# The delta rule's output projection starts in the branch's own pool, and the output weights load in another order

## The chip, the cores and the metric

The kernel runs on one NeuronCore of one Trainium2 chip. The core has a matrix engine (TensorE; its weight loads are listed apart as PEld), a vector engine (VectorE, in the profile DVE), a scalar engine (ScalarE, ACT), GpSimd (POOL) and a sync engine (SP), which issues the DMA transfers here. TensorE writes its sums into PSUM banks of 128 x 512 float32. The metric is the time of one execution on the device in microseconds; 2331.53 us is the median of three runs before the change (2330.88 to 2333.11).

## The reference

Two layers of a decoder trunk over 512 tokens of width 1024, in float32. Each layer normalises x and feeds three branches side by side: a Mamba-2 state space branch, a latent attention (MLA) and a gated delta rule (GDN). Each branch's result is projected to the model width and gated, the three are added and projected once more, and a feed-forward part follows:

```
mixed = g_ssd * (y_ssd @ w_ssd_out) + g_mla * (y_mla @ w_mla_out) + g_gdn * (y_gdn @ w_gdn_out)
h = x + mixed @ w_out
f = jnp.square(jax.nn.relu(rmsnorm(h, norm2_g) @ w_up)) @ w_down
return h + f
```

The gates are sigmoids of a projection of the normalised x. The change touches `g_gdn * (y_gdn @ w_gdn_out)`, `mixed @ w_out` and, through a shared helper, the product with `w_down`.

## The kernel before, in words

**Products.** A float32 operand is split into a high part, rounded to fp32r, and a low rest; three matmuls (L182 high by high, L183 low by high, L184 high by low, or the other way round) make one product. `weights` loads a weight block of 512 KB into one of two buffers `wraw` (L161) and splits it 512 columns at a time, on ScalarE (L154, `whi`) and VectorE (L155, `wlo`), into a ring of four pairs. One such pair feeds 12 matmuls of 512 columns where two feature tiles are computed. `dense_F` runs one product with the features on the partitions: it takes one bank for each of its two feature tiles from the four accumulation banks `acc`.

**The branches.** In order of the text come the state space groups, the attention's projection in between, the delta rule's matrices, the state space branch's projection (`out_proj`), and two calls of `gdn_unit`, each for four heads. A unit walks four chunks of 128 tokens: a chain that alternates between TensorE (L1004 to L1042), VectorE (L1008 to L1045), ScalarE (L1051) and GpSimd (the power of L259) and ends with four multiplies on VectorE into the tile `gz` (L1063; its buffers have the tag `tok`). After the four chunks, four features are transposed one after another through a single bank (`y_bank`, L1068) and split into `yh` and `yl` (L254, L255), the operands of the delta rule's projection.

**`out_proj`** goes over pairs of feature tiles, `dp` 0 to 3. For each pair it computes the gate logits (`dense_F` of `xh`, `xl` with a slice of w_in), takes a tanh of each bank into a gate tile (L464), computes the branch's projection (`dense_F` of `yh`, `yl` with w_gdn_out), multiplies it on to the gate tile (L473) and adds that to `mixed` (L474). The gate tile is a buffer `cva` of the given pool, or what `make` gives; with `make`, L473 and L474 have a raised priority.

**Pools over one another.** The branches' tiles lie in the pool `br`, closed after the second unit. The pools `hp` (the residual `h`, 2 MB) and `wo` (the output product) are opened afterwards over the same memory; a tile in them waits until the tiles of `br` that it overlaps have been read for the last time. Before the change all of the delta rule's projection comes behind that point: pairs 0 to 2 at once, with gate tiles in places of `wo` and `hp` that are not in use yet (`slots`), and pair 3 inside the output product (`mid`).

**The output product.** `seven` multiplies with w_out (and later four times per layer with w_down) as 2 x 2 blocks with seven block products (Strassen's scheme in Winograd's form): a11, a12, s2, s1, s3, s4, a22. `seven_weights` gives the four blocks of 1 MB, `wr00`, `wr01`, `wr11` and `wr10`, loaded by `after(c)` for c = 0, 1, 2, 3 in that order (L1113), and two sums of blocks on VectorE (L1107): `wp1` = block 00 + block 01, and block 01 += block 11. Each sum is two additions of 128 x 1024. A third sum (L1159) builds the operand of the product s2 from `wp1` and block 11, a fourth (L1170) that of a22. For w_down, `after(c)` is called behind the c-th of four column groups of the up projection.

**Order.** A planner orders each engine's instructions ahead of time: it goes through a simulated time and takes the instruction that comes first in the text among those that are ready and have a buffer, or one of raised priority. It can so take an instruction well ahead of its place in the text. On the chip each engine, and the DMA queue of SP, then works through its list in that fixed order.

Of the kernel before, what the change touches and what calls it, by code (L numbers as in the profile page):

```python
# [55 lines left out]
def hybrid_kernel(ctx, tc, a, out, depth=2, taps=None):  # L56
# [108 lines left out]
    def weights(w2d, c0, n, K, hold=None, raw0=None):  # L165

        kt = min(1024 // n, K // P)  # L170
        step = 512 // n
        for k0 in range(0, K // P, kt):
            given = raw0 is not None and k0 == 0
            raw = raw0 if given else weights_raw(w2d, c0, n, k0, kt)
            for q in range(0, kt, step):
                hi, lo = split_half(raw[:, q * n : (q + step) * n], hold and hold[k0 + q], not given)
                v = lambda x: x.rearrange("p (k n) -> p k n", n=n)
                yield k0 + q, v(hi), v(lo)
# [7 lines left out]
    def dense_F(gen, cols, K, xh, xl, mid=None, banks=None, after=None):  # L186

        pss = banks or [acc_bank() for _ in cols]
        last = K // P - 1
        if mid:
            gen = list(gen)
            for i, hf in enumerate(HALVES):
                for ps, c in zip(pss, cols):
                    for k0, wh, wl in gen:
                        for k in range(wh.shape[1]):  # L200
                            kk = k0 + k
                            mm3(ps[:, hf], wh[:, k, c], wl[:, k, c], xh[kk][:, hf], xl[kk][:, hf], kk == 0, kk == last)
                if i == 0:
                    mid()
            return pss
        for k0, wh, wl in gen:
            for ps, c in zip(pss, cols):
                for k in range(wh.shape[1]):
                    a_, b_ = wh[:, k, c], wl[:, k, c]
                    mm3(ps[: a_.shape[1], :], a_, b_, xh[k0 + k], xl[k0 + k], k0 + k == 0, k0 + k == last)  # L210
            if after:
                after()
        return pss
# [110 lines left out]
    hpl = h_pool.enter_context(tc.tile_pool(name="hp", bufs=1, reuse_waits="tile"))  # L324
# [26 lines left out]
    for ly in range(depth):  # L351
# [107 lines left out]
        def out_proj(w2d, br, yh, yl, pl, part=range(4), after=None, make=None, gate_banks=lambda: None):  # L459
            for dp in part:  # L460
                tg = []
                for j, ps in enumerate(dense_F(weights(w_in, O_GATE + br * D + dp * 256, 256, D), tiles(256), D, xh, xl, None, gate_banks(), after)):
                    t_ = make(dp, j) if make else mk(pl, [P, S], F32, "cva", 2)
                    act.activation(t_, ps, AF.Tanh, scale=0.5)  # L464
                    tg.append(t_)
                for j, ps in enumerate(dense_F(weights(w2d, dp * 256, 256, D), tiles(256), D, yh, yl, after=after)):
                    d = 2 * dp + j
                    if mixed[d] is None:
                        mixed[d] = mk(lp, [P, S], F32, "mix", 8)
                        dve.scalar_tensor_tensor(mixed[d], tg[j], 1.0, ps, ALU.add, ALU.mult)  # L470
                    else:
                        with tc.high_priority() if make else nullcontext():
                            dve.scalar_tensor_tensor(tg[j], tg[j], 1.0, ps, ALU.add, ALU.mult)  # L473
                            dve.tensor_tensor(mixed[d], mixed[d], tg[j], ALU.add)  # L474
# [224 lines left out]
        br = bp.enter_context(tc.tile_pool(name="br", bufs=1, reuse_waits="tile"))  # L699
# [391 lines left out]
        yg = hilo_tags(lp, "y")  # L1091
        for u in range(2):
            gdn_unit(u, *mats[u], *yg)
        bp.close()


        h_pool = ExitStack()
        hpl = h_pool.enter_context(tc.tile_pool(name="hp", bufs=1, reuse_waits="tile"))
        last = ly == depth - 1
        ssq = [mk(sp, [P, 2], F32, "nss", 4) for _ in range(T)]  # L1100
        def seven_weights(pl, w2d, r0):

            b = {}

            def plus(o, x, y):
                for q in (slice(0, 1024), slice(1024, 2048)):
                    dve.tensor_tensor(o[:, q], x[:, q], y[:, q], ALU.add)  # L1107

            def after(c):
                i, j = ((0, 0), (0, 1), (1, 1), (1, 0))[c]  # L1110
                b[i, j] = mk(pl, [P, 4 * 512], F32, f"wr{i}{j}")
                rows, cols = (slice(o + 512 * e, o + 512 * (e + 1)) for o, e in ((r0, i), (0, j)))
                sync.dma_start(b[i, j].rearrange("p (k n) -> p k n", k=4), w2d[rows, cols].rearrange("(k p) n -> p k n", p=P))  # L1113
                if c == 1:
                    b["p1"] = mk(pl, [P, 4 * 512], F32, "wp1")
                    plus(b["p1"], b[0, 0], b[0, 1])
                if c == 2:
                    plus(b[0, 1], b[0, 1], b[1, 1])

            return b, after  # L1120
# [59 lines left out]
            product(x, "a22", of(p4), False, 1, 0, ALU.add, 2)  # L1180

        with tc.tile_pool(name="wo", bufs=1, reuse_waits="tile") as wo:
            slots = {(0, 0): (wo, "wr00"), (0, 1): (hpl, "h"), (1, 0): (wo, "wr10"), (1, 1): (wo, "wp1"),
                     (2, 0): (wo, "wr01"), (2, 1): (wo, "wr11"), (3, 0): (wo, "fs"), (3, 1): (wo, "fs")}

            def gate_tile(dp, j):
                pl, tag = slots[dp, j]
                return mk(pl, [P, S], F32, tag, 2 if tag == "fs" else 1)

            out_proj(a["w_gdn_out"][ly], 2, *yg, wo, (0, 1, 2), make=gate_tile)  # L1190
            h = mk(hpl, [P, T, D], F32, "h")
            for t in range(T):
                sync.dma_start(h[:, t, :], xsrc[t * P : (t + 1) * P, :])
            hts = [h[:, t] for t in range(T)]
            b, after = seven_weights(wo, a["w_out"][ly], 0)
            for c in (0, 3, 1, 2):
                after(c)
            ops = {}
            ck_pair = lambda: list(zip(*hilo_tags(lp, "ck", 2)))
            ops["a11"], ops["s3"] = ck_pair(), list(zip(*hilo_tags(wo, "s3", 2)))  # L1200

            def mid():
                out_proj(a["w_gdn_out"][ly], 2, *yg, wo, (3,), make=gate_tile, gate_banks=lambda: [sm_bank() for _ in range(2)])
                fh, fl = hilo_tags(lp, "x")
                for i, n in enumerate(("a12", "s2", "s1", "s4")):
                    ops[n] = [(fh[2 * i + e], fl[2 * i + e]) for e in range(2)]
                ops["a22"] = ck_pair()

            def put(n, d, s):
                hi, lo = (x[:, d % 2 * 256 : d % 2 * 256 + 256] for x in ops[n][d // 2])  # L1210
                act.mul(hi, s, 0.5)
                dve.scalar_tensor_tensor(lo, s, 0.5, f32(hi), ALU.mult, ALU.subtract)

            def comb(x, y, op):
                s = mk(wo, [P, 256], F32, "fc", 8)
                dve.tensor_tensor(s, x, y, op)
                return s

            half = lambda i: lambda d: mixed[d][:, HALVES[i]]
            t0, t1 = half(0), half(1)  # L1220

            held = []

            def forms(n):
                for d in range(4):
                    with tc.high_priority() if d > 1 and n in ("a12", "s2") else nullcontext():
                        form(n, d)

            def form(n, d):
                if n == "a11":  # L1230
                    put("a11", d, t0(d))
                    put("s3", d, comb(t0(d), t1(d), ALU.subtract))
                if n == "a12":
                    put("a12", d, t0(d + 4))
                if n == "s2":
                    s = comb(t1(d), t1(d + 4), ALU.subtract)
                    s2 = comb(s, t0(d), ALU.subtract)
                    put("s2", d, s2)
                    held.append((s, s2))
                if n == "s1":  # L1240
                    s, s2 = held[d]
                    put("s1", d, s)
                    put("s4", d, comb(t0(d + 4), s2, ALU.add))
                if n == "a22":
                    put("a22", d, t1(d + 4))

            nf = []

            def n2(i, pl, *tag):
                if not nf:  # L1250
                    nf.extend(hilo_tags(lp, "x"))
                norm_half(i, hts, ssq, lambda k: col(g_n2 + k), pl, *nf, *tag)

            seven(wo, ops, b, ssq, lambda: n2(0, wo, "f", 2), nf=2, pre=forms, mid=mid)
            xh, xl = nf
# [138 lines left out]
```

## Time and profile before

| | |
|---|---|
| median of three runs | 2331.53 us |
| the profiled execution | 2332.37 us |
| its span, first to last instruction | 2330.6 us |
| mean granted TensorE clock | 0.993 |
| TensorE busy | 2280.6 us |
| VectorE busy | 1647.8 us |
| ScalarE busy | 1201.1 us |

The profile has one execution. A row of the timeline gives start, duration, engine, line, operation, written and read tiles, their shapes and the number of instructions merged, and in brackets the idle time of the engine just before and what ended it. A row of the waits gives the engine and line that waited, what released it, the total in us, the number of times and the longest. A row of the windows gives the window, its length, then busy time and number of instructions of PE, PEld, DVE, ACT and POOL, the granted clock of TensorE as a share of full speed, the busy share of the DMA engines and their GB/s.

### The profile page before, as it was taken

The numbers are of one execution on the slowest core, as the hardware profiler recorded it, in microseconds if no ns is written. First come the engines' busy times: TensorE is split into PE (matmuls) and PEld (weight loads), VectorE is DVE, ScalarE is ACT, GpSimd is POOL, SyncE is SP. The second block draws the span as 40 slices with busy tenths as digits, with TensorE's granted clock in tenths as the row PEclk, the third lists the DMA queues.
The fourth block names the chain that finished last, engine by engine and source line by source line (L and its number), as shares of the span: only waits on it lengthen the run. The fifth ranks groups of instructions, "written<-read, shape, count | busy, mean of one in ns | idle before, by whom it ended". The sixth has DMA issues, their size and how long they took to land.

```text
span 2330.6 us, 32281 instructions
## 1 busy us (share of the span) xinstructions
PE 2280.6 (98%) x11810; PEld 1873.1 (80%) x11810; DVE 1647.8 (71%) x3256; ACT 1201.1 (52%) x2509; POOL 59.5 (3%) x74
## 2 busy tenths in 40 slices
PE   9999999999998999999999999999999999999998
PEld 7888787878887888888888877878788778888886
DVE  7777566866665868767867775668657649778668
ACT  6666744333443455554657666443344335545545
POOL 0000000000000000000000000000000100000000
PEclk9999999999999999999999999999999989999999
DMA  4223633442224233233132236334422242432231
GB/s 141 79 73 100 191 100 116 145 119 82 79 67 136 90 136 109 82 109 118 52 97 78 78 108 190 100 109 145 119 82 82 63 136 73 145 117 100 91 109 46
DMA packets 220032, 244.16 MB, mean 105 GB/s; under 512 B 34256, under 2 KB 172384, under 8 KB 219872
## 3 DMA queue, kind: packets, MB, share of 16 engines
q1 hardware_dynamic: 219872, 242.09, 34.0%
q8 instruction: 93, 1.52, 0.3%
q14 instruction: 67, 0.55, 0.1%
HBM read 225.60 MB, written 11.74 MB: 102 GB/s over the span
## 4 chain that ended last, share of the span: by engine, by line
PE 87%; DVE 7%; ACT 2%; issue 1%; POOL 1%; DMA 1%; SPq 0%; DVEq 0%; POOLq 0%; ACTq 0%
PE acc L182 22%; PE acc L183 22%; PE acc L184 22%; PE sm L184 2%; PE sm L182 2%; PE sm L183 2%; DVE wlo L155 2%; PE sm L752 1%; DVE tok L880 1%; ACT whi L154 1%; PE sm L650 1%; DVE gQ L879 1%; PE sm L1037 1%; POOL gms L259 1%; PE sm L761 1%
## 5 line engine op out<-in xcount | busy, mean ns | idle before, releaser
L155 DVE TENSOR_TENSOR wlo<-wraw,whi 128x512 fp32r<-128x512 f32 (+1 forms) x536 | 366.1, 686 | 363.5 <-ACT whi L154 358.0
L154 ACT CAST whi<-wraw 128x512 fp32r<-128x512 f32 (+1 forms) x536 | 330.2, 618 | 555.5 <-PE acc L183 380.5
L182 PE MATMUL acc<-xh,whi 128*128 128x512 f32 (+1 forms) x1344 | 522.7, 390 | 0.7 <-ACT xh L254 0.7
L184 PE MATMUL acc<-xh,wlo 128*128 128x512 f32 (+1 forms) x1344 | 523.1, 390 | 0.0
L183 PE MATMUL acc<-xl,whi 128*128 128x512 f32 (+1 forms) x1344 | 522.8, 389 | 0.3 <-DVE xl L255 0.3
L183 PEld LDWEIGHTS acc<-xl,whi 128*128 128x128 f32 x1344 | 253.4, 189 | 48.4 <-DVE xl L255 1.1
L182 PEld LDWEIGHTS acc<-xh,whi 128*128 128x128 f32 x1344 | 252.5, 188 | 49.4 <-ACT xh L254 1.5
L184 PEld LDWEIGHTS acc<-xh,wlo 128*128 128x128 f32 x1344 | 253.4, 189 | 47.5
L154 ACT CAST whi<-wr 128x512 fp32r<-128x512 f32 x168 | 104.4, 621 | 111.0 <-PE acc L183 50.1
L182 PE MATMUL acc<-yh,whi 128*128 128x512 f32 x384 | 152.6, 401 | 1.6 <-ACT yh L254 1.6
L183 PE MATMUL acc<-yl,whi 128*128 128x512 f32 x384 | 153.3, 399 | 0.0
L184 PE MATMUL acc<-yh,wlo 128*128 128x512 f32 x384 | 151.5, 394 | 0.0
L155 DVE TENSOR_TENSOR wlo<-wr,whi 128x512 fp32r<-128x512 f32 x168 | 113.5, 687 | 33.9 <-ACT whi L154 33.1
L691 DVE SCALAR_TENSOR_TENSOR ckl<-acc,pc,ckl 128x511 f32<-128x511 f32 (+2 forms) x168 | 120.3, 743 | 15.5 <-ACT ckl L687 8.2
L182 PEld LDWEIGHTS acc<-yh,whi 128*128 128x128 f32 x384 | 72.9, 191 | 17.3 <-ACT yh L254 2.6
L184 PEld LDWEIGHTS acc<-yh,wlo 128*128 128x128 f32 x384 | 73.1, 190 | 14.6
L183 PEld LDWEIGHTS acc<-yl,whi 128*128 128x128 f32 x384 | 73.4, 191 | 14.0
L183 PE MATMUL acc<-wlo,xh 128*128 128x512 f32 (+1 forms) x208 | 80.1, 385 | 0.0
L184 PE MATMUL acc<-whi,xl 128*128 128x512 f32 (+1 forms) x208 | 79.7, 385 | 0.0
L182 PE MATMUL acc<-whi,xh 128*128 128x512 f32 (+1 forms) x208 | 79.2, 382 | 0.0
L1144 DVE TENSOR_TENSOR h<-h,acc 128x512 f32<-128x512 f32 x120 | 77.2, 681 | 0.2 <-PE acc L184 0.2
L454 ACT ACTIVATE eE<-eE,cum 128x128 f32<-128x128 f32 x192 | 63.2, 390 | 24.6 <-DMA eE<-d_c 19.7
(455 smaller groups left out, 4560.9 us busy)
## 6 DMA issues: line engine op xcount, KB each, us to landing
wraw<-in_w_in_dram SPq DMA_DIRECT2D x144, 512.0 KB, 3.6
wraw<-in_w_up_dram SPq DMA_DIRECT2D x64, 512.0 KB, 3.6
wr<-in_w_down_dram SPq DMA_DIRECT2D x32, 1024.0 KB, 5.3
eE<-d_c SPq DMA_DIRECT2D x48, 256.0 KB, 3.7
wraw<-in_w_mla_out_dram SPq DMA_DIRECT2D x16, 512.0 KB, 3.4
eE<-d_e SPq DMA_DIRECT2D x32, 256.0 KB, 2.8
wraw<-in_w_ssd_out_dram SPq DMA_DIRECT2D x16, 512.0 KB, 3.3
wraw<-in_w_gdn_out_dram SPq DMA_DIRECT2D x16, 512.0 KB, 3.4
```

The lines of the kernel that those rows point to most:

```text
L154: act.copy(hi, raw)
L155: dve.tensor_tensor(lo, raw, f32(hi), ALU.subtract)
L182: pe.matmul(o, ah, bh, start=start, stop=False, skip_group_check=more)
L183: pe.matmul(o, ah, bl, start=False, stop=False, skip_group_check=more)
L184: pe.matmul(o, al, bh, start=False, stop=stop, skip_group_check=more)
L259: pool.tensor_tensor(o, o, (exp if exp is not None else nhalf)[:, : o.shape[1]], ALU.pow)
L454: act.activation(o[:, i], o[:, i], AF.Relu, scale=-1.0, bias=cum[:, t, h0 + i : h0 + i + 1])
L650: pe.transpose(ps[:, n : n + P], pn[t][:, kb * P : (kb + 1) * P], ident)
L691: dve.scalar_tensor_tensor(acc[:, d:], ps[:, : S - d], taps_[3 - d], acc[:, d:], ALU.mult, ALU.add)
L752: pe.matmul(py[64 * i : 64 * i + 64, c * P : (c + 1) * P], xd[:, t, h * 64 : (h + 1) * 64], e2[h // 4][:, h % 4, :], start=True, stop=True)
L761: pe.matmul(po[:, c * P : (c + 1) * P], st[:, c * P : (c + 1) * P], ctl[:, tok], start=True, stop=True)
L1144: dve.tensor_tensor(hs_, hs_, ps[t], op)
```

## The change

The first pair of the delta rule's projection (dp = 0) is computed ahead of the closing of the branch's pool, with its gate tiles in the branch's `cva` buffers and without raised priority. Pairs 1 and 2 stay behind it and get other places for their gate tiles. The blocks of w_out are loaded in the order 00, 01, 11, 10 (before: 00, 10, 01, 11). In `seven_weights`, for w_out and w_down, both sums are written one load later.

```diff
         for u in range(2):
             gdn_unit(u, *mats[u], *yg)
+        out_proj(a["w_gdn_out"][ly], 2, *yg, br, (0,))
         bp.close()
...
-                if c == 1:
+                if c == 2:
                     b["p1"] = mk(pl, [P, 4 * 512], F32, "wp1")
                     plus(b["p1"], b[0, 0], b[0, 1])
-                if c == 2:
+                if c == 3:
                     plus(b[0, 1], b[0, 1], b[1, 1])
...
-            slots = {(0, 0): (wo, "wr00"), (0, 1): (hpl, "h"), (1, 0): (wo, "wr10"), (1, 1): (wo, "wp1"),
-                     (2, 0): (wo, "wr01"), (2, 1): (wo, "wr11"), (3, 0): (wo, "fs"), (3, 1): (wo, "fs")}
+            slots = {(1, 0): (wo, "wr11"), (1, 1): (hpl, "h"), (2, 0): (wo, "wr10"), (2, 1): (wo, "fs"),
+                     (3, 0): (wo, "fs"), (3, 1): (wo, "fs")}
...
-            out_proj(a["w_gdn_out"][ly], 2, *yg, wo, (0, 1, 2), make=gate_tile)
+            out_proj(a["w_gdn_out"][ly], 2, *yg, wo, (1, 2), make=gate_tile)
...
-            for c in (0, 3, 1, 2):
+            for c in range(4):
                 after(c)
```

## The prediction

> **What bounds the kernel now.** I read the busy shares first, then who waited for whom on TensorE, then the order of time around the one large wait, and last the windows.
>
> ```profile
> PE 2280.6 (98%) x11810; PEld 1873.1 (80%) x11810; DVE 1647.8 (71%) x3256; ACT 1201.1 (52%) x2509; POOL 59.5 (3%) x74
> PE yt L1068 <- DVE tok L1063: 9.2, 4, 4.1
> PE sm L1037 <- issue: 3.0, 2, 1.5
> ```
>
> TensorE is busy 98% of the span, so 50 us of idle is all there is, and its largest wait sits where the delta rule's last transposes (L1068) wait for VectorE. It comes once per layer at 4.1 us (the 9.2 us hold two more, small ones). Two windows per layer, in each pair layer 0 first: the tail of the delta rule, and all that follows up to the second norm.
>
> ```profile
> 708.44:726.20 17.76, 11.40 (x47) 8.67 (x46) 7.86 (x20) 5.86 (x16) 1.01 (x1) 0.81 0.09 31
> 1861.05:1880.03 18.98, 12.62 (x47) 9.32 (x46) 7.86 (x20) 5.85 (x16) 1.01 (x1) 0.64 0.08 28
> 726.20:828.68 102.48, 102.48 (x451) 84.22 (x450) 74.27 (x135) 47.05 (x96) 0.96 (x2) 1.00 0.36 118
> 1880.03:1982.50 102.47, 102.46 (x451) 84.24 (x450) 74.19 (x135) 47.16 (x96) 0.97 (x2) 1.00 0.36 118
> ```
>
> In the tail TensorE idles 17.76 - 11.40 = 6.36 us and again 18.98 - 12.62 = 6.36 us, at a mean granted clock of 0.81 and 0.64. Afterwards it has no gap for 102 us, one matmul per 102.48/451 = 227 ns. So the change can win only in the tail, and behind it can only lose. The tail of layer 0 in order of time, TensorE first, then ScalarE, VectorE and the DMA queue:
>
> ```profile
> 696.36 0.48 PE L184 MATMUL acc<-xh,wlo 128*128 128x512 f32 x1
> 696.67 0.40 PE L182 MATMUL acc<-yh,whi 128*128 128x512 f32 x1
> 707.62 0.49 PE L1018 MATMUL sm<-tok,tok 128*128 128x128 f32 x2 [0.41 <-DVE tok L1015]
> 709.94 1.13 PE L1037 MATMUL sm<-wk,eE 128*128 128x128 f32 x8 [1.50 <-issue]
> 716.03 0.33 PE L1068 MATMUL yt<-ct,tok 128*128 128x128 f32 x1 [4.09 <-DVE tok L1063]
> 717.13 1.22 PE L182 MATMUL acc<-yh,whi 128*128 128x512 f32 x2 [0.78 <-ACT yh L254]
> 726.20 0.42 PE L182 MATMUL acc<-xh,whi 128*128 128x512 f32 x1
> ...
> 699.21 0.62 ACT L1025 ACTIVATE wk<-sm,gcd 128x128 f32<-128x128 f32 x2 [3.09 <-DVE wk L1020]
> ...
> 723.71 0.62 ACT L154 CAST whi<-wraw 128x512 fp32r<-128x512 f32 x1 [0.36 <-PE acc L183]
> 725.47 0.59 ACT L464 ACTIVATE wr<-acc 128x512 f32<-128x512 f32 x1
> 725.95 0.60 ACT L464 ACTIVATE h<-acc 128x512 f32<-128x512 f32 x1
> ...
> 708.55 0.69 DVE L155 TENSOR_TENSOR wlo<-wraw,whi 128x512 fp32r<-128x512 f32 x1
> ...
> 686.40 11.63 SPq L161 DMA_DIRECT2D wraw<-in_w_in_dram  x2
> 709.27 0.37 SPq L161 DMA_DIRECT2D wraw<-in_w_gdn_out_dram  x1
> ```
>
> Pair 0's gate products (from xh) end at 696.36 and its projection products (from yh) start at 696.67; the half of them that needs only the first unit's rows fills the delta rule's steps until 708. Then TensorE has nothing it may do. Pair 1's gate weights are there: both loads were issued by 698, and the load at 709.27, into the slot of the first of them, shows its two splits done (the second ends at 708.55 + 0.69). What is missing is banks. Pair 0's gate sums sit in two of the four accumulation banks from 696.8 until their tanh at 725.47 and 725.95, because those tanh write into tiles (wr00, h) that lie over the branch's tiles, which the last transposes still read; the projection holds the other two. Pair 1's first gate matmul starts at 726.20, right behind the first tanh.
>
> **The change part by part.**
>
> *Pair 0's gate tiles in the branch's pool.* Nothing is added: the same 48 + 48 matmuls, 2 tanh, 2 fused multiplies and 2 adds, in two buffers (cva) that the branch has already. Moved is the tanh, some 28 us earlier (to 697, where ScalarE idles 3.09 us ahead of 699.21), and two banks come free there. Pair 1's gate products can then fill the tail: 48 x 0.227 = 10.9 us of work. The tail's loss is its idle time and its slow clock:
>
> ```profile
> 709.50:712.90 3.40, 2.00 (x12) 1.57 (x12) 1.19 (x5) 1.05 (x4) 0.00 (x0) 1.00 0.46 159
> 712.90:716.40 3.50, 0.33 (x1) 0.14 (x1) 1.71 (x9) 0.81 (x7) 1.01 (x1) 1.00 0.01 2
> 716.40:723.10 6.70, 5.97 (x18) 4.85 (x19) 1.86 (x4) 1.81 (x3) 0.00 (x0) 0.50 0.00 0
> 1859.94:1863.35 3.41, 1.62 (x11) 1.34 (x12) 2.51 (x7) 0.55 (x1) 0.00 (x0) 0.99 0.11 30
> 1863.35:1877.00 13.65, 8.79 (x26) 6.47 (x26) 4.42 (x14) 3.74 (x12) 1.01 (x1) 0.50 0.09 31
> ```
>
> Idle: 6.36 + 6.36 = 12.7 us. Half clock: half of the busy time in it, 5.97/2 + 8.79/2 = 7.4 us. Together 20.1 us, 10 per layer, and 10.9 us of filler stand against it. The second half of the filler must be split inside the tail: its raw block has landed, a ring place comes free when the first 12 matmuls are done, and ScalarE is busy 5.86 of 17.76 us, VectorE 7.86.
>
> The order of the queues is fixed by a planner, so the fill won't be exact. Where filler was at hand it fell short by 0.41 us (the row at 707.62). I take that at four places per layer, ahead of L1037, of the first transposes, of the first product behind them and once among the later transposes: 8 x 0.45 = 3.6 us stays. Expected gain 20.1 - 3.6 = 16.5 us. Bounds: 20.1 us if all goes; nothing if the planner doesn't fill.
>
> On the clock, row and page differ. In layer 0 it fell behind a window with 0.33 of 3.50 us busy and held through one with 2.00 of 3.40; in layer 1 it fell behind one with 1.62 of 3.41 busy. So half empty is enough here, and the fill must be dense. The Trainium skill ("TensorE: Matmul & The Clock Gate", Part 1: The HAM clock gate) states that the clock halves after an idle window of about 3.4 us; layer 1 had no such idle time before 1863.35, so the trace agrees only in part. With a dense fill both give the same sum.
>
> *No raised priority* for pair 0's two multiplies and adds (4 x 0.69 us on VectorE): they gate pair 1's projection banks, but pair 1's leftover gate matmuls, 10.9 - 10 = 0.9 us, and the other two banks stand ahead. Between 0 and 0.9 us late per layer; I take 0, as the idle share of VectorE in the tail is over half.
>
> *The tiles move on.* Pair 1 now gets wr11 and h, pair 2 wr10 and fs. Their tanh still wait for the branch's tiles, and then the projection of pair 0 is through anyway. The residual's load into h now waits for pair 1, not pair 0, and block 11 of w_out too; blocks 00 and 01 wait for no gate, block 10 for pair 2.
>
> ```profile
> 734.66 1.45 SPq L1193 DMA_DIRECT2D h<-in_x_dram  x3
> 770.98 2.17 SPq L1113 DMA_DIRECT2D wr<-in_w_out_dram  x2
> 775.04 3.49 SPq L161 DMA_DIRECT2D wraw<-in_w_gdn_out_dram  x2
> 730.00:740.00 10.00, 10.00 (x46) 8.29 (x45) 5.36 (x11) 4.56 (x9) 0.00 (x0) 1.00 0.95 315
> 750.31 0.68 DVE L474 TENSOR_TENSOR mix<-mix,wp 128x512 f32<-128x512 f32 x1
> 776.25 1.28 DVE L1144 TENSOR_TENSOR h<-h,acc 128x512 f32<-128x512 f32 x2
> ```
>
> The residual goes out 16 us later, at 751 on the old clock (pair 1's last add is at 750.31), 2 MB and a block of 1 MB at 315 GB/s land by 761, and the first use is at 776.25: hidden. Queued behind them on the DMA queue are the weights of pair 2's projection. Four splits of 12 matmuls stand ahead of TensorE, 4 x 2.72 = 10.9 us; the burst needs 3 MB/315 = 10 us and the weights 3.4 more. Between 0 and 2.5 us per layer; I take 0, since two such blocks ahead of weights (770.98, then 775.04) cost TensorE nothing.
>
> *The sums one load later.* 40 additions of 1.22 us, 4 per product, none more or fewer:
>
> ```profile
> 778.05 2.35 DVE L1107 TENSOR_TENSOR wp<-wr,wr 128x1024 f32<-128x1024 f32 x2
> 770.00:780.00 10.00, 10.00 (x46) 8.29 (x45) 9.97 (x18) 4.47 (x9) 0.00 (x0) 1.00 0.78 267
> 917.23 1.23 DVE L1107 TENSOR_TENSOR wp<-wr,wr 128x1024 f32<-128x1024 f32 x1
> 924.85 1.21 DVE L1107 TENSOR_TENSOR wr<-wr,wr 128x1024 f32<-128x1024 f32 x1
> 940.00:950.00 10.00, 10.00 (x46) 8.29 (x45) 4.63 (x7) 5.35 (x9) 0.00 (x0) 1.00 0.29 95
> 970.00:980.00 10.00, 10.00 (x45) 8.09 (x45) 9.96 (x18) 5.77 (x10) 0.00 (x0) 1.00 0.01 5
> ```
>
> For w_out they sit in a full VectorE (9.97 of 10); with 00 and 01 loaded early they can go ahead of it. That costs or wins nothing, since TensorE has no gap there. For w_down they are written behind the second column group but run at 917 to 925, long before it; one group later in the text, VectorE still has 5 of 10 us free at 940. Cost 0.
>
> **Sum.** The profiled execution took 2332.37 us, 1.8 beyond its span and 0.84 above the median. 2332.37 - 16.5 = 2315.9; on the median's footing 2315.0.
>
> **The rivals.**
>
> *The fill is thin.* Only pair 1's first 12 matmuls slip in, 2.7 us per layer, the rest is planned behind the projection. Then over half of the long wait stays empty and, by the layer 1 row, the clock still falls: gain 5.4 us, 2326; with 24 matmuls 10.9 us, 2320.6. For it: the tail's splits compete with the chain on VectorE. Against: 24 matmuls are ready at 709. By the page's rule the clock would hold once no window is empty, and then 12 matmuls give 5.4 + 7.4 = 12.8 us, 2318.7. Chance 0.15, a third of it with the clock held.
>
> *Nothing moves.* The tanh is planned late for another reason, the banks stay taken: 2331.5. Against: ScalarE's idle time there. Chance 0.08.
>
> *Slower: w_down's sums are late.* If the four additions of a product (4.9 us) run where VectorE is full (9.96 of 10), TensorE waits for the operand built from them in the third product: about 4.9 us less some 2 us of slack, 3 us, in 8 products, 24 us. 2315 + 24 = 2339. It decides from the sixth product on (6 x 3 > 16.5). Against it: the old ones run some 20 us ahead of their place in the text, as soon as their blocks land. Chance 0.13, with whatever else a new plan upsets.
>
> **How the numbers follow.** The likeliest, a dense fill, has 0.64 and its own range 2310 to 2320 (all 20.1 us, or 5 us lost at the DMA queue). The range reaches over the thin fill to 2326, which holds 0.79. What a measurement can tell from no change is about 0.2%, 4.7 us: faster 0.64 + 0.15 = 0.79, same 0.08, slower 0.13.
>
> **What would show it.** Right: two tanh into cva some 28 us ahead of the last transposes; matmuls acc<-xh inside the tail; the 4.1 us wait gone; the clock at 1.00 there; the next 102 us without gaps as before. Wrong: the tanh early but acc<-xh still behind the last transposes (thin fill); gaps with a wait for wraw loads near the residual's load (the queue); L1107 in the windows with a full VectorE and gaps in the third product (the sums).

## The result, and the profile after

The changed kernel takes 2314.54 us (median of 4, 2313.46 to 2314.88), the kernel before 2332.32 us over the runs beside it. The ratio is 0.9922, with a 95% interval of 0.9905 to 0.9939. The profiled execution has a span of 2313.1 us, 17.5 less than before.

The first line of the page shows the same 11810 matmuls, 7.9 us less of TensorE's busy time, and VectorE as before:

```profile
PE 2272.7 (98%) x11810; PEld 1866.7 (81%) x11810; DVE 1647.6 (71%) x3256; ACT 1200.5 (52%) x2509; POOL 59.5 (3%) x74
```

The stage to look at runs from the last solve product of the last chunk (the last L1018) to the first transpose of the second norm: the tail and all that the change moves behind it. Its windows, before the change, then after it, each time layer 0 and layer 1 (window, length, then busy us and instructions of PE, PEld, DVE, ACT, POOL, the granted clock, the DMA share and GB/s):

```profile
707.83:829.12 121.29, 114.49 (x499) 93.20 (x499) 83.17 (x157) 52.94 (x112) 2.38 (x3) 0.97 0.32 104
1860.44:1982.93 122.49, 115.69 (x500) 93.87 (x499) 83.09 (x157) 53.06 (x112) 2.39 (x3) 0.94 0.31 103
```

```profile
706.20:819.09 112.89, 111.53 (x499) 90.87 (x498) 82.92 (x157) 51.75 (x110) 2.39 (x3) 1.00 0.33 112
1852.48:1965.36 112.88, 111.53 (x499) 90.88 (x499) 82.96 (x157) 51.72 (x110) 2.39 (x3) 1.00 0.33 112
```

The stage is 8.40 us shorter in layer 0 and 9.61 us in layer 1, 18.0 together; all other stages together are 0.5 us longer in this execution. The 18.0 us are two terms. Idle time of TensorE falls from 6.80 to 1.36 and from 6.80 to 1.35 us, 10.9 us in all. Its busy time falls by 2.96 and 4.16 us, 7.1 in all, for the same number of matmuls, with the clock at 1.00 in place of 0.97 and 0.94.

The timeline of the tail after the change, TensorE, then ScalarE and the DMA queue, shows what fills it. The line that the change adds shifts later line numbers by one (L1193 is L1194 here).

```profile
706.66 0.39 PE L182 MATMUL acc<-xh,whi 128*128 128x512 f32 x1
...
708.48 1.05 PE L1037 MATMUL sm<-wk,eE 128*128 128x128 f32 x8
...
713.66 0.39 PE L184 MATMUL acc<-xh,wlo 128*128 128x512 f32 x1
715.02 0.33 PE L1068 MATMUL yt<-ct,tok 128*128 128x128 f32 x1 [0.97 <-DVE tok L1063]
...
692.49 0.60 ACT L464 ACTIVATE cva<-acc 128x512 f32<-128x512 f32 x1 [1.44 <-PE acc L184]
695.24 0.60 ACT L464 ACTIVATE cva<-acc 128x512 f32<-128x512 f32 x1 [0.75 <-PE acc L184]
728.58 0.59 ACT L464 ACTIVATE wr<-acc 128x512 f32<-128x512 f32 x1
...
741.02 1.77 SPq L1194 DMA_DIRECT2D h<-in_x_dram  x4
```

Both tanh of pair 0 run before 696. Pair 1's gate matmuls start at 706.66, ahead of L1037 and not behind the last transposes: 24 of the 48 run there until 714 (8 ahead of L1037, 16 behind L1042), the others from 715 on between the transposes and the projection. Of the 4.09 us wait 0.97 us is left; the waits ahead of L1037 and ahead of the first projection matmul behind the transposes are gone. The residual's load goes out at 741, behind pair 1.

### The profile page after: what moved, and what is told of

Read it like the earlier page. It is cut to its first block, busy times and chain, and to the rows that moved or that the text cites. A ratio compares the mean times of both kernels' runs of the same rounds, so it can differ in the third digit from the quotient of the medians.

```text
span 2313.1 us, 32290 instructions
## 1 busy us (share of the span) xinstructions
PE 2272.7 (98%) x11810; PEld 1866.7 (81%) x11810; DVE 1647.6 (71%) x3256; ACT 1200.5 (52%) x2509; POOL 59.5 (3%) x74
## 4 chain that ended last, share of the span: by engine, by line
PE 86%; DVE 8%; ACT 2%; DMA 2%; POOL 1%; issue 1%; SPq 0%; DVEq 0%; POOLq 0%; ACTq 0%
PE acc L182 22%; PE acc L183 21%; PE acc L184 21%; PE sm L184 2%; PE sm L183 2%; PE sm L182 2%; DVE wlo L155 2%; PE sm L752 1%; ACT whi L154 1%; DVE tok L880 1%; PE sm L650 1%; DVE gQ L879 1%; PE sm L1037 1%; POOL gms L259 1%; PE yt L666 1%
```

## The experiments

Each kernel was timed beside the kernel before; the edits are against the kernel before.

**The move alone.** The old order of the blocks, the old place of the sums, the old gate tiles of pairs 1 and 2:

```diff
         for u in range(2):
             gdn_unit(u, *mats[u], *yg)
+        out_proj(a["w_gdn_out"][ly], 2, *yg, br, (0,))
         bp.close()
...
-            out_proj(a["w_gdn_out"][ly], 2, *yg, wo, (0, 1, 2), make=gate_tile)
+            out_proj(a["w_gdn_out"][ly], 2, *yg, wo, (1, 2), make=gate_tile)
```

> Theory (banks): the move of pair 0 alone, with the old order of w_out's blocks, the old places of the sums and the old tiles for pairs 1 and 2, gives all of the gain, 17 to 18 us, so 2314 to 2315. Rival (loads and sums): part of the gain comes from the blocks loaded in another order and the later sums; then this stays at 2318 or more. Other rival: the new places cost a little and this is faster than the changed kernel, below 2313.

Measured: 2315.16 us, ratio 0.9925 (0.9911 to 0.9939). The stage as above:

```profile
707.28:820.13 112.85, 111.49 (x499) 90.80 (x498) 82.61 (x157) 51.77 (x110) 2.39 (x3) 1.00 0.34 112
1851.71:1964.56 112.85, 111.47 (x500) 90.80 (x499) 82.74 (x157) 51.66 (x110) 2.39 (x3) 1.00 0.34 112
```

The stage has the changed kernel's length to 0.04 us in both layers. The move gives the whole gain, to what can be told here.

**The rest alone.** The new load order and the later sums, all three pairs behind the closing of the pool, in their old tiles:

```diff
-                if c == 1:
+                if c == 2:
...
-                if c == 2:
+                if c == 3:
...
-            for c in (0, 3, 1, 2):
+            for c in range(4):
```

> Theory (banks): the load order and the later sums alone, with all of pairs 0 to 2 behind the closing of the branch's pool, change nothing: within 2 us of before, and the 4.1 us wait of the last transposes stands. Rival (loads and sums): 3 us or more faster. Rival (late sums hurt): 3 us or more slower, with gaps of TensorE in w_down's products.

Measured: 2332.17 us against 2332.68, ratio 0.9998 (0.9989 to 1.0007). TensorE's waits in the window of layer 0 (who waited for whom, total us, times, longest), then the stage in both layers:

```profile
PE yt L1068 <- DVE tok L1063: 4.1, 1, 4.1
PE sm L1037 <- issue: 1.5, 1, 1.5
...
705.45:826.72 121.27, 114.50 (x499) 93.10 (x498) 83.10 (x157) 53.05 (x112) 2.39 (x3) 0.97 0.31 105
1858.23:1980.94 122.71, 115.89 (x499) 93.77 (x499) 83.02 (x157) 52.97 (x112) 2.39 (x3) 0.96 0.32 103
```

The waits and the length of the stage are those of the kernel before, to 0.2 us. The load order and the sums are worth nothing that this measurement can tell.

**The place of the tiles alone.** Nothing moves in the text; pair 0's two gate tiles get memory that lies over no tile of the branch:

```diff
-            slots = {(0, 0): (wo, "wr00"), (0, 1): (hpl, "h"), (1, 0): (wo, "wr10"), (1, 1): (wo, "wp1"),
+            slots = {(0, 0): (lp, "ckh0"), (0, 1): (lp, "ckh1"), (1, 0): (wo, "wr10"), (1, 1): (wo, "wp1"),
```

> Theory (banks): nothing is moved in the text, pair 0 stays behind the closing of the branch's pool and keeps its raised priority; only its two gate tiles get memory that lies over no tile of the branch (the free tiles ckh0 and ckh1). Then the tanh can run early just the same, pair 1's gate products fill the tail, and the gain is the same 17 to 18 us. Rival (place in the text): the order in which the work is written, ahead of the pool's closing, is what lets the planner fill; then this stays near 2331.

Measured: 2318.27 us, ratio 0.9934 (0.9920 to 0.9947), some 3.7 us above the changed kernel's median, in other runs on another occasion. The stage, both layers:

```profile
710.95:823.83 112.88, 111.50 (x499) 90.79 (x499) 82.61 (x157) 51.76 (x110) 2.39 (x3) 1.00 0.34 112
1856.10:1968.93 112.83, 111.49 (x499) 90.82 (x498) 82.59 (x157) 51.75 (x110) 2.39 (x3) 1.00 0.34 112
```

The stage is that of the changed kernel, although out_proj stands where it stood. So it is the place of the tiles, not the place in the text, that lets the tanh run and the banks come free. The profiled executions of the two kernels are 3.4 us apart, and that lies outside the stage: it begins at 710.95 here and at 706.20 in the changed kernel. Ahead of it this execution has 13.66 us at half clock, and the changed kernel's has none (it has 3.42 us later, between the two stages):

```profile
11.37:14.78 3.41, 3.41 (x14) 3.41 (x15) 2.87 (x8) 2.50 (x8) 0.55 (x1) 0.50 0.56 148
65.98:69.40 3.42, 3.42 (x10) 2.65 (x9) 2.92 (x7) 1.64 (x4) 0.99 (x1) 0.50 0.00 0
506.30:513.13 6.83, 6.83 (x83) 5.32 (x76) 3.77 (x7) 4.92 (x10) 0.00 (x0) 0.50 0.98 220
```

Both kernels were run once more, side by side.

> The kernel of e3_place_only once more, beside the changed kernel on one chip. Theory (the tail is the same, the 3 us between e3_place_only and the changed kernel are the clock's phase in other stages): within 2 us of the changed kernel here. Rival (the two tiles ckh0 and ckh1, or the raised priority, cost something): again 3 to 4 us slower than the changed kernel.

> The changed kernel itself, as the other half of e6_place_again: 2313 to 2316 where before is 2331 to 2333.

Measured: 2315.38 us for the place alone (0.9930, 0.9916 to 0.9945), 2317.21 us for the changed kernel (0.9932, 0.9919 to 0.9945), beside 2333.56 for before. This time the changed kernel is the slower one, by 1.8 us, and its median lies above what was expected of it. The stage is 112.86 and 112.88 us long in the two, so the difference isn't in it. They are the same to what can be told here.

**One bank free.** Only the first of the two gate tiles gets free memory; the second stays in `h`:

```diff
-            slots = {(0, 0): (wo, "wr00"), (0, 1): (hpl, "h"), (1, 0): (wo, "wr10"), (1, 1): (wo, "wp1"),
+            slots = {(0, 0): (lp, "ckh0"), (0, 1): (hpl, "h"), (1, 0): (wo, "wr10"), (1, 1): (wo, "wp1"),
```

> As e3_place_only for the first gate tile alone; the second stays over the branch's tiles. Theory (banks): one bank comes free, half of pair 1's gate products may run there, and of those the 12 that fit in the ring of split weights: 8 ahead of L1037, 4 ahead of the last transposes, 2.7 us per layer. By the row of layer 1 (the clock fell behind a window about half empty) the clock still halves: gain 5 to 6 us, 2326. If it takes a whole empty window of 3.4 us, the clock holds: gain 5.4 + 7.4 = 12.8 us, 2319. Rival (all or nothing, both banks are needed): 2331.

Measured: 2324.63 us, ratio 0.9966 (0.9955 to 0.9977), 8.0 us below before. Tail of layer 0 on TensorE, then windows: the last one at full clock and the slow one behind it, layer 0 and layer 1, then the stage.

```profile
711.07 0.40 PE L182 MATMUL acc<-xh,whi 128*128 128x512 f32 x1
715.09 0.47 PE L1068 MATMUL yt<-ct,tok 128*128 128x128 f32 x1 [3.15 <-DVE tok L1063]
...
711.40:714.81 3.41, 0.53 (x3) 0.09 (x1) 1.62 (x9) 1.28 (x8) 1.01 (x1) 1.00 0.01 2
714.81:721.63 6.82, 5.76 (x18) 4.45 (x19) 2.51 (x6) 1.37 (x2) 0.00 (x0) 0.50 0.45 154
1861.70:1865.10 3.40, 0.30 (x2) 0.00 (x0) 1.61 (x9) 1.14 (x8) 1.01 (x1) 1.00 0.00 0
1865.10:1871.90 6.80, 5.97 (x18) 4.65 (x19) 2.29 (x5) 1.37 (x2) 0.00 (x0) 0.50 0.44 154
...
706.78:825.40 118.62, 114.28 (x500) 92.83 (x499) 82.81 (x157) 52.57 (x111) 2.38 (x3) 0.97 0.33 107
1856.84:1975.59 118.75, 114.38 (x499) 92.91 (x498) 82.86 (x157) 52.45 (x111) 2.39 (x3) 0.97 0.33 107
```

One of the two banks gives part of the fill. The stage gains 2.67 us in layer 0, where 12 matmuls are 12 x 0.227 = 2.72 us and the slow clock stays as long as before. In layer 1 it gains 3.74 us: the same 2.7 and 1.0 more, since the slow stretch there is 6.80 and not 13.65 us long. The wait ahead of the transposes is still 3.15 us and the clock halves in both layers: of the two ways in which the clock could go, the first came true. The 0.53 and 0.30 us busy in the windows ahead don't tell whether a quite empty window is needed.

**Idle time and clock apart.** The kernel before, with work that nobody uses in the hole:

```diff
                 sn = None
+                tail = u == 1 and t == T - 1
+                if tail:
+                    idle = sm_bank()
+                    for i in range(6):
+                        pe.matmul(idle, xh[i][:, :P], xh[i], start=True, stop=True)
...
+                    for i in range(14 if tail else 0):
+                        pe.matmul(idle, xh[i % 8][:, :P], xh[i % 8], start=True, stop=True)
                     act.copy(o, po)
```

> The kernel before with 20 matmuls of 512 columns per layer added in the last chunk of the second unit, 6 ahead of L1037 and 14 behind L1042, into a bank that nobody reads. Their 20 x 0.227 = 4.5 us per layer lie in the tail's idle time and do no work of the product. Theory (idle time and clock are two terms): the idle term stays lost, the clock holds in both layers, gain up to 7.4 us, so 2325 to 2329. Rival (the slow clock costs nothing of its own, since the chain through VectorE and ScalarE sets the tail): 2332 as before. Other rival (the chain is on TensorE too, the added matmuls push it back): 2334 to 2341.

Measured: 2326.64 us beside 2333.56 before, ratio 0.9977 (0.9967 to 0.9987), faster with 40 matmuls more. The ratio, over all runs, is a gain of 5.4 us; the medians are 6.9 us apart. The windows of 3.4 us at the old hole, one per layer, and the stage:

```profile
710.80:714.20 3.40, 2.41 (x11) 1.44 (x9) 1.61 (x9) 1.33 (x6) 1.01 (x1) 1.00 0.00 0
1861.10:1864.50 3.40, 2.43 (x13) 1.65 (x11) 1.61 (x9) 1.56 (x8) 1.01 (x1) 1.00 0.00 0
705.92:825.11 119.19, 116.78 (x520) 94.27 (x519) 82.98 (x157) 53.54 (x112) 2.39 (x3) 1.00 0.32 106
1856.62:1975.85 119.23, 116.85 (x520) 94.27 (x519) 82.89 (x157) 53.64 (x112) 2.38 (x3) 1.00 0.32 106
```

The clock holds at 1.00 with 2.4 of 3.4 us busy, and the stage is 2.10 and 3.26 us shorter, 5.4 us in all. No useful work was won for the hole: the six projection matmuls that run in it made room for six useless ones in the steps ahead. The slow clock is a term of its own, as taken in the sum; here it is worth 5.4 us where the sum had 7.4 and the changed kernel wins 7.1. Most of what is missing is busy time of TensorE: 111.53 us, as in the changed kernel, and 20 matmuls of 0.227 would be 116.07, and 116.78 and 116.85 are measured. Why they take longer isn't shown.

## Why the prediction was right

*The mechanism.* It named the banks held by two tanh that wait for the branch's tiles, and pair 1's gate products as what would fill the tail. The place of the tiles alone gives the same stage, to 0.1 us, and one tile alone gives its 12 matmuls. So runs show bank, tile and fill; they are not only argued.

*The sizes.* Expected were 12.7 us of idle time less 3.6 that stay, 9.1 us, and 7.4 us of clock: 16.5. Measured were 10.9 and 7.1 us: 18.0 in the stage. The remainder of the idle time was taken too high. Four places of 0.45 us per layer were assumed; of the three waits over 0.5 us in each tail only the one ahead of the first transposes was left, with 0.97 and 0.94 us. In the profiled executions the account closes: 2332.37 - 18.0 + 0.5 for the other stages is 2314.9, and 2314.88 was measured. By the medians the gain is 17.8 us where 16.5 were forecast. That the forecast of 2315.0 lies only 0.5 us from 2314.54 is partly luck, since it stood on 2331.53 us for the kernel before, which took 2332.32 beside the changed kernel.

*What is left of the wait.* Half of the 0.97 us comes from the filler itself. The products of L1042 and the first transposes are 5.12 us apart before the change (710.91 and 716.03) and 5.65 us after it (709.37 and 715.02), since ScalarE now splits a weight block for pair 1 in the middle of the chain's L1051. Layer 1 has the same split at 1857.50; with one tile free there is no split at that place, and the two are 5.12 us apart again (709.97 and 715.09). The prediction looked for this competition on VectorE only.

```profile
710.91 1.03 PE L1042 MATMUL sm<-st,ft 128*128 128x256 f32 x4
```

```profile
709.37 1.03 PE L1042 MATMUL sm<-st,ft 128*128 128x256 f32 x4
...
711.20 0.60 ACT L154 CAST whi<-wraw 128x512 fp32r<-128x512 f32 x1
711.71 0.30 ACT L1051 ACTIVATE gk<-wk 128x128 f32<-128x128 f32 x1
```

*The tanh* came where it was said: the stage begins 1.63 us earlier in the changed kernel's execution, so the second one, at 695.24, is at 696.9 on the old clock. The first, at 692.49, came still earlier, since the first bank's sums end before the second's.

*What was costed at nothing.* The residual's load went out at 741.02, right behind pair 1's last add, as said; everything there is 10 us earlier than before, so this is the 751 of the old clock, and the first use is at 766. The blocks and the weights behind it cost TensorE nothing, for the windows behind the tail have no gap. Nor did the missing raised priority: the place alone keeps it, and its stage is as long to 0.1 us. The windows:

```profile
728.41:818.60 90.19, 90.19 (x397) 74.07 (x396) 69.25 (x127) 43.30 (x90) 0.91 (x2) 1.00 0.36 125
1874.67:1964.90 90.23, 90.23 (x398) 74.08 (x396) 69.34 (x127) 43.28 (x90) 0.94 (x2) 1.00 0.36 125
```

The sums for w_out run at 741 to 747, ahead of the stretch with a full VectorE, and win nothing there. Those for w_down, which the slower rival needed late, run in the second round at 907 to 915, 10 us earlier than before like everything around them:

```profile
740.91 2.35 DVE L1108 TENSOR_TENSOR wp<-wr,wr 128x1024 f32<-128x1024 f32 x2
907.20 1.23 DVE L1108 TENSOR_TENSOR wp<-wr,wr 128x1024 f32<-128x1024 f32 x1
914.81 1.22 DVE L1108 TENSOR_TENSOR wr<-wr,wr 128x1024 f32<-128x1024 f32 x1
```

So the text moved and the plan did not. What sums that are really late would cost was not tried.

*The thin fill* was priced at 5.4 us with a falling clock for 12 matmuls. The kernel with one tile is that case: 6.4 us in the stage, 8.0 in the medians.

## What to carry to other kernels

Where TensorE waits for a chain and other products are ready, ask what they lack: here it was two PSUM banks, held 30 us by evacuations whose target lay over tiles still in use. Give such an evacuation memory of its own; where it stands in the text didn't matter here. Price a hole on TensorE by its idle time and by the slow clock behind it, here 10.9 and 7.1 us.

## What the runs showed of the hardware that was not expected

The clock did not need an empty window to halve. In the nine traces of this case it halves and returns only at steps of 3.41 us (slow stretches of 3.41, 6.83 and 13.65 us), and the step ahead of a fall was often about half busy. Three such steps: from the kernel before, one with 1.76 us busy of 3.41, shown with the half clock behind it, and one with 1.84 of 3.40 that no half clock followed; from the changed kernel one with 2.24 of 3.40, in a stretch of small matmuls, again with the half clock behind it.

```profile
501.39:504.80 3.41, 1.76 (x68) 1.29 (x66) 0.15 (x1) 1.19 (x2) 0.00 (x0) 1.00 1.02 161
504.80:508.22 3.42, 3.42 (x47) 2.48 (x47) 1.39 (x2) 2.47 (x5) 0.00 (x0) 0.50 1.11 195
706.20:709.60 3.40, 1.84 (x10) 1.13 (x8) 2.53 (x9) 0.62 (x1) 0.90 (x1) 1.00 0.00 0
```

```profile
1206.05:1209.45 3.40, 2.24 (x18) 1.92 (x18) 1.79 (x6) 1.50 (x3) 0.86 (x1) 1.00 0.35 115
1209.45:1212.87 3.42, 3.42 (x9) 2.64 (x9) 2.36 (x5) 1.78 (x4) 1.12 (x1) 0.50 0.00 0
```

In these traces the clock fell behind every step that was less than half busy, away from the kernel's first ten microseconds. Of the steps with a busy share between 0.52 and 0.75 it fell behind six and held behind the others; busy time as the profile has it doesn't separate these. Where the steps fall against the work differs from one execution to the next, and with it whether a wait of 1.7 to 1.9 us at 502 costs nothing, one slow step or two.

Each timed run has its mean granted clock on record, and in the sets whose times spread by more than 2 us the longer runs have the lower clock: the changed kernel's second set goes from 2313.11 us at 0.999 to 2320.45 us at 0.995, the place alone from 2314.70 at 0.998 to 2319.55 at 0.995. A thousandth of the clock over 2315 us is 2.3 us, so the clock is enough to account for this spread. That may also be why the same kernel's medians differ by 3 us from one set of runs to the next (2314.54 and 2317.21 for the changed kernel, 2318.27 and 2315.38 for the place alone); the clocks on record, given to a thousandth, are too coarse to show it, and the timed runs have no trace.
